# DeltaNet's 8x8 substitution on GpSimd instead of VectorE, and two weights' low halves on VectorE instead of GpSimd

## The chip, the cores and the metric

The kernel runs on one core of one Trainium2 chip. The metric is the device time of one execution in microseconds (us), the median over runs. The core's engines work side by side and wait for each other through semaphores: TensorE (PE, matrix products into PSUM), VectorE (DVE), ScalarE (ACT), GpSimd (POOL) and SyncE (SP), which issues the transfers from memory.

## The reference

A two-layer decoder over 272 tokens (16 learned ones and 256 of input), width 1024. Each layer is a half-step FFN, a mixer and another half-step FFN. The mixer projects its input once and splits the columns among three head groups: stick-breaking attention, gated DeltaNet and an S5 state-space group with a gated output (GLU). Cut to the part that the change touches, DeltaNet solves, for every head and chunk of tokens, a unit lower triangular system:

```
lmat  = where(strict, einsum('bhnid,bhnjd->bhnij', kb, kc) * decay, 0.0)
t_inv = triangular_solve(lmat + eye, eye, left_side=True, lower=True, unit_diagonal=True)
u = t_inv @ (vc * beta);   w = t_inv @ (kb * exp(gc))
attn = where(incl, (qc @ kc^T) * decay, 0.0)
# then over the chunks, in sequence: v_new = u - w S;  o = q exp(g) S + attn v_new
#                                    S = S exp(g_last) + (k exp(g_last - g))^T v_new
h += concat(o_sb, o_dn, o_s5) @ w_out
```

## The kernel before

**Products in three parts.** A weight tile comes from memory as fp32 (`raw`). `weights` (lines 127 to 141) makes a high half `wh` on ACT (L136) and a low half `wl = raw - wh` by one subtraction of 128x1024 (L139), on VectorE, or on GpSimd if the weight's number within the mixer is in `ON_POOL` (line 47). `mm3` (L144 to L146) adds three products: `wh xh`, `wh xl` and `wl xh`. A unit of the projection is 8 blocks of 3 products, 24 matmuls of 128x272.

**The mixer** (`mixer`). In the order in which it is run: the units of the convolution's columns (`conv`), of `s5u`, `z`, `q`, `k`, `v`. VectorE takes each unit out of PSUM (L1343, L1358, L1364). Meanwhile `dn_gates` makes DeltaNet's triangular matrices `LT`, and `s5` runs the state-space scan in four groups: PE gives `pinc` (L821), VectorE rotates, scans and rotates back (L825 to L839), and GpSimd clears the first column (L837) once L836 is done. When the projections are through come the attention's scores (`pz`, L1227 to L1231), DeltaNet's second set of products (`pl`, L887) and transposes (`pv`), S5's outputs (`pY`, L850 and L852), the GLU (`pglu`), the rest of the attention (L1242 to L1257) and the output projection.

**The inverse** (`dn_inverse`). Nine sets of four 8x8 diagonal blocks stand in each column of partitions. One product with `bd8` (`pl8` and `pl8t`, L992 and L994) spreads each block's entries over its partitions, ACT copies them out of PSUM as `Lb` (L996, L997). Then the 8x8 blocks are inverted by substitution: seven steps, each a product (L1005) and a subtraction (L1006) that needs the step before; L1008 spreads the result into 32x32 tiles `TT32`, and VectorE transposes them (L1010, `T32`). Two levels of block doubling follow, each `px` (L1016), a copy, `py` (L1022), a subtraction (L1024) and a transpose (L1025); then 32 to 64 (`px2`, `py2`, L1033 to L1054) and 64 to 128 (L1060 to L1071). Only then can `dn_rest` run its sequence over the chunks (`pvn` L1138, `pS` L1143 and L1145, `pk` L1129 and L1130).

**What sets the order.** The program is written in Python order with priorities (`first()` puts DeltaNet ahead of all, `second()` the GLU); a scheduler then orders the instructions of each engine once, when the kernel is built, by its own estimate of times. On the chip each engine takes its instructions strictly in that order: an instruction that must wait holds up all behind it.

Of the kernel before, what the change touches and what calls it, by code (L numbers as in the profile page):

```python
# [14 lines left out]
ALU = mybir.AluOpType  # L15
# [3 lines left out]
P = 128  # L19
# [24 lines left out]
HORD = (0, 1, 4, 2, 5, 3, 8, 6, 7, 9)  # L44
SA, SB = 1, 1
CONV, UORD, ZK = (0, 1, 4, 5), (0, 1, 2, 3), 0
ON_POOL = (5, 7, 10, 15, 20, 25)
NBUF = (3, 2, 3)
LO_POOL = 5

# [5 lines left out]
def bc(ap, axis, n):  # L56
    return ap.unsqueeze(axis).to_broadcast([*ap.shape[:axis], n, *ap.shape[axis:]])
# [6 lines left out]
class Trunk:  # L64
# [17 lines left out]
    def psum(self, tag, nm):  # L82

        return self.ps.tile([P, 512], F32, tag=tag, name=nm, bufs=2)
# [885 lines left out]
    def dn_inverse(self):  # L970

        nc = self.nc
        V, G, A, PE = nc.vector, nc.gpsimd, nc.scalar, nc.tensor
# [17 lines left out]
        p = psum("pl8")  # L991
# [3 lines left out]
        Lb = self.m1024("Lb")[:, :576]  # L995
        A.copy(Lb[:, :512], p)  # L996
        A.copy(Lb[:, 512:], p2[:, :64])  # L997
        Lb = Lb.rearrange("p (u i j) -> p u i j", u=9, i=8)
# [1 line left out]
        for k in range(2):  # L1000
            G.tensor_tensor(Lm[k], L32, bc(self.lev[k], 1, 9), op=ALU.mult)
        TT8, t8 = tl([P, 9, 8], "TT8"), tl([P, 9, 8], "t8")
        V.tensor_copy(TT8, bc(self.id8, 1, 9))
        for j in range(7):
            V.tensor_tensor(t8[:, :, j + 1:], Lb[:, :, j + 1:, j], TT8[:, :, j:j + 1].to_broadcast([P, 9, 7 - j]), op=ALU.mult)  # L1005
            V.tensor_tensor(TT8[:, :, j + 1:], TT8[:, :, j + 1:], t8[:, :, j + 1:], op=ALU.subtract)  # L1006
        TT32, T32 = t9("TT32"), t9("T32")
        V.tensor_tensor(TT32.rearrange("p u (b i) -> p u b i", b=4), bc(TT8, 2, 4),  # L1008
                        bc(self.m8c.rearrange("p (b i) -> p b i", b=4), 1, 9), op=ALU.mult)
        V.transpose(fl(T32), fl(TT32))  # L1010

        for k in range(2):
# [10 lines left out]
            Tn, TT32 = t9("T32"), t9("TT32")  # L1023
# [293 lines left out]
    def mixer(self, l, nxt):  # L1317
# [7 lines left out]
        R = self.R  # L1325
        self.on_pool, self.nw = ON_POOL, -1
        with ExitStack() as es:
# [167 lines left out]
```

## Time and profile before

| | us |
|---|---|
| median of 3 runs | 1191.51 (1189.88 to 1191.59) |
| profiled execution, its own time | 1194.31 |
| its span, first to last instruction | 1192.5 |
| PE busy in the span | 1154.8 (97%) |
| VectorE busy | 853.6 (72%) |
| ScalarE busy | 614.1 (52%) |
| GpSimd busy | 175.3 (15%) |

The mixer of layer 0 stands at about 227 to 410 us of the span, that of layer 1 at about 815 to 1000 us. The share of busy time is a mean over stages with different limits; the two mixers are where PE waits or runs at a low clock, and the windows below are taken from them.

### The profile page before, as it was taken

The numbers are of one execution on the slowest core, as the hardware profiler recorded it, in microseconds if no ns is written. First come the engines' busy times: TensorE is split into PE (matmuls) and PEld (weight loads), VectorE is DVE, ScalarE is ACT, GpSimd is POOL, SyncE is SP. The second block draws the span as 40 slices with busy tenths as digits, with TensorE's granted clock in tenths as the row PEclk, the third lists the DMA queues.
The fourth block names the chain that finished last, engine by engine and source line by source line (L and its number), as shares of the span: only waits on it lengthen the run. The fifth ranks groups of instructions, "written<-read, shape, count | busy, mean of one in ns | idle before, by whom it ended". The sixth has DMA issues, their size and how long they took to land.

```text
span 1192.5 us, 23762 instructions
## 1 busy us (share of the span) xinstructions
PE 1154.8 (97%) x9544; PEld 1104.5 (93%) x9544; DVE 853.6 (72%) x1648; ACT 614.1 (52%) x981; POOL 175.3 (15%) x210
## 2 busy tenths in 40 slices
PE   8999999999998999999999999999999989999997
PEld 7999999998786999999999999999988969999985
DVE  7999986699636866555579998756994268666644
ACT  6455575564166654444455556645632566555533
POOL 6312100021010111110201112011210001111100
PEclk9999999999789999999999999999997599999999
DMA  5656545543201455555565555455431015666663
GB/s 182 179 175 180 166 135 160 167 125 108 71 19 54 142 175 177 168 176 171 177 187 177 169 173 172 132 175 156 124 112 33 27 45 185 181 188 191 187 191 117
DMA packets 196858, 173.74 MB, mean 146 GB/s; under 512 B 21300, under 2 KB 193004, under 8 KB 196748
## 3 DMA queue, kind: packets, MB, share of 16 engines
q1 hardware_dynamic: 196732, 172.22, 48.2%
q8 instruction: 75, 1.23, 0.4%
q14 instruction: 35, 0.29, 0.1%
q10 hardware_dynamic: 16, 0.00, 0.0%
HBM read 171.15 MB, written 1.05 MB: 144 GB/s over the span
## 4 chain that ended last, share of the span: by engine, by line
PE 84%; DVE 10%; ACT 3%; issue 1%; DMA 1%; SPq 0%; ACTq 0%; DVEq 0%
PE proj L146 17%; PE proj L145 17%; PE proj L144 17%; PE pd L146 5%; PE pd L145 5%; PE pd L144 5%; PE pd L493 5%; DVE wl L139 2%; PE pY L852 1%; DVE qkv L1346 1%; DVE xT L1437 1%; PE pY L850 1%; PE pl L887 1%; PE pm L783 1%; PE pz L1227 1%
## 5 line engine op out<-in xcount | busy, mean ns | idle before, releaser
L144 PE MATMUL proj<-xh,wh 128*128 128x272 f32 (+1 forms) x1840 | 521.1, 289 | 6.3 <-DVE sy L1435 2.8
L145 PE MATMUL proj<-xl,wh 128*128 128x272 f32 (+1 forms) x1840 | 518.4, 287 | 0.2 <-DVE xl L1296 0.2
L146 PE MATMUL proj<-xh,wl 128*128 128x272 f32 (+1 forms) x1840 | 492.8, 290 | 3.3 <-DVE wl L139 3.0
L136 ACT ACTIVATE wh<-raw 128x1024 fp32r<-128x1024 f32 (+1 forms) x324 | 338.2, 1044 | 292.8 <-PE proj L145 99.5
L139 DVE TENSOR_TENSOR wl<-raw,wh 128x1024 fp32r<-128x1024 f32 (+1 forms) x312 | 378.4, 1213 | 146.6 <-PE pd L146 60.9
L144 PEld LDWEIGHTS proj<-xh,wh 128*128 128x128 f32 x1840 | 345.4, 188 | 10.5 <-DVE sy L1435 4.1
L145 PEld LDWEIGHTS proj<-xl,wh 128*128 128x128 f32 x1840 | 345.2, 188 | 3.0 <-issue 1.5
L146 PEld LDWEIGHTS proj<-xh,wl 128*128 128x128 f32 x1840 | 328.8, 187 | 7.2 <-DVE wl L139 5.8
L144 PE MATMUL pd<-hh,wh 128*128 128x272 f32 x528 | 149.6, 288 | 0.0
L145 PE MATMUL pd<-hl,wh 128*128 128x272 f32 x528 | 149.3, 288 | 0.0
L435 POOL TENSOR_TENSOR hl<-h,hh 128x272 fp32r<-128x272 f32 (+1 forms) x88 | 81.1, 924 | 452.9 <-ACT hh L434 452.8
L146 PE MATMUL pd<-hh,wl 128*128 128x272 f32 x528 | 140.8, 288 | 0.2
L144 PEld LDWEIGHTS pd<-hh,wh 128*128 128x128 f32 x528 | 99.2, 188 | 0.2
L145 PEld LDWEIGHTS pd<-hl,wh 128*128 128x128 f32 x528 | 99.3, 188 | 0.1
L146 PEld LDWEIGHTS pd<-hh,wl 128*128 128x128 f32 x528 | 95.1, 188 | 1.0 <-DVE wl L139 0.9
L107 ACT ACTIVATE g<-g 128x272 f32<-128x272 f32 (+2 forms) x92 | 37.6, 415 | 68.9 <-DVE g L429 68.8
L433 DVE TENSOR_TENSOR h<-proj,g 128x272 f32<-128x272 f32 (+1 forms) x88 | 37.7, 433 | 32.9 <-PE proj L146 21.3
L434 ACT ACTIVATE hh<-h 128x272 fp32r<-128x272 f32 (+1 forms) x88 | 36.4, 419 | 47.1 <-DVE h L433 47.1
L429 DVE TENSOR_TENSOR g<-proj,R 128x272 f32<-128x272 f32 (+1 forms) x88 | 37.5, 430 | 17.8 <-PE proj L146 17.6
L139 POOL TENSOR_TENSOR wl<-raw,wh 128x1024 fp32r<-128x1024 f32 x12 | 30.7, 2557 | 110.5 <-ACT th L107 34.9
L431 DVE TENSOR_TENSOR g<-g,R 128x272 f32<-128x272 f32 (+1 forms) x88 | 37.7, 432 | 12.6 <-ACT g L107 12.3
L376 POOL TENSOR_TENSOR acc<-acc,sq 128x272 f32<-128x272 f32 (+1 forms) x20 | 22.7, 1134 | 91.4 <-ACT sq L370 90.5
(490 smaller groups left out, 1310.1 us busy)
## 6 DMA issues: line engine op xcount, KB each, us to landing
raw<-in_ffn_w_gate_dram SPq DMA_DIRECT2D x88, 512.0 KB, 3.6
raw<-in_ffn_w_up_dram SPq DMA_DIRECT2D x88, 512.0 KB, 3.6
raw<-in_ffn_w_down_dram SPq DMA_DIRECT2D x70, 512.0 KB, 3.5
raw<-in_w_in_dram SPq DMA_DIRECT2D x36, 512.0 KB, 4.4
raw<-in_ffn_w_down_dram SPq DMA_DIRECT2D x24, 384.0 KB, 3.0
raw<-in_w_out_dram SPq DMA_DIRECT2D x16, 512.0 KB, 3.5
raw<-in_s_w_glu_dram SPq DMA_DIRECT2D x4, 512.0 KB, 3.4
xin<-in_x_dram SPq DMA_DIRECT2D x4, 256.0 KB, 5.8
```

The costliest lines, as they stand in the source:

```text
L107: i = self.nc.scalar.activation(out, in_, func, **k)
L136: nc.scalar.activation(h[:, :n], r[:, :n], AF.Copy)
L139: e.tensor_tensor(l[:, :n], r[:, :n], f32(h[:, :n]), op=ALU.subtract)
L144: mm(p, wh, xh, start=first, stop=False)
L145: mm(p, wh, xl, start=False, stop=False)
L146: mm(p, wl, xh, start=False, stop=last)
L429: V.tensor_tensor(g1, pg[j][:, :N], R, op=ALU.mult)
L431: V.tensor_tensor(g1, g1, R, op=ALU.mult)
L433: V.tensor_tensor(h, pu[j][:, :N], g1, op=ALU.mult)
L434: nc.scalar.activation(hh[:, f, :N], h, AF.Copy)
L435: G.tensor_tensor(hl[:, f, :N], h, f32(hh[:, f, :N]), op=ALU.subtract)
L493: PE.matmul(pd[i][e], x[:, f, ts], w[:, 0, e * 512:e * 512 + 512], start=f == 0 and w is h and x is hh, stop=f == NF - 1 and w is lo)
```

## The change

The substitution's 16 instructions per layer (the copy of the unit matrix, seven products, seven subtractions, and the spreading into 32x32 tiles) are issued on GpSimd instead of VectorE. The transpose that follows stays on VectorE. The weights 10 and 15 of each mixer (the first unit of `z`, and the second of `k`) leave `ON_POOL`, so that their low halves are made on VectorE. All lines from 1003 on move by one: L1005 of before is L1006 of the changed kernel, L1010 is L1011, L1016 is L1017.

```
-ON_POOL = (5, 7, 10, 15, 20, 25)
+ON_POOL = (5, 7, 20, 25)
...
-        V.tensor_copy(TT8, bc(self.id8, 1, 9))
+
+        G.tensor_copy(TT8, bc(self.id8, 1, 9))
         for j in range(7):
-            V.tensor_tensor(t8[:, :, j + 1:], Lb[:, :, j + 1:, j], TT8[:, :, j:j + 1].to_broadcast([P, 9, 7 - j]), op=ALU.mult)
-            V.tensor_tensor(TT8[:, :, j + 1:], TT8[:, :, j + 1:], t8[:, :, j + 1:], op=ALU.subtract)
+            G.tensor_tensor(t8[:, :, j + 1:], Lb[:, :, j + 1:, j], TT8[:, :, j:j + 1].to_broadcast([P, 9, 7 - j]), op=ALU.mult)
+            G.tensor_tensor(TT8[:, :, j + 1:], TT8[:, :, j + 1:], t8[:, :, j + 1:], op=ALU.subtract)
         TT32, T32 = t9("TT32"), t9("T32")
-        V.tensor_tensor(TT32.rearrange("p u (b i) -> p u b i", b=4), bc(TT8, 2, 4),
+        G.tensor_tensor(TT32.rearrange("p u (b i) -> p u b i", b=4), bc(TT8, 2, 4),
                         bc(self.m8c.rearrange("p (b i) -> p b i", b=4), 1, 9), op=ALU.mult)
         V.transpose(fl(T32), fl(TT32))
```

The scheduler orders every engine anew. Three places, all in the mixer of layer 0 (layer 1 reads the same but for numbers):

GpSimd's queue, as a difference (`s5z_3954` is the first S5 group's state, `s5z_3981` the second's):

```order
 L837 MEMSET s5z_3954 128x8
-L139 TENSOR_TENSOR wl<-raw,wh 128x1024
+L1006 TENSOR_TENSOR t_3313<-Lb,TT_3312 128x9x7
+L1007 TENSOR_TENSOR TT_3312<-TT_3312,t_3313 128x9x7
+L1006 TENSOR_TENSOR t_3313<-Lb,TT_3312 128x9x6
...
+L1007 TENSOR_TENSOR TT_3312<-TT_3312,t_3313 128x9
+L1009 TENSOR_TENSOR TT_3329<-TT_3312,m8c 128x288
 L837 MEMSET s5z_3981 128x8
```

The 15 instructions stand in one piece behind the clearing of the first S5 group's column, and nothing stands between them.

VectorE's queue around the transpose that closes the substitution, before (`pv` is the last unit of the projection, the rotations are those of the fourth S5 group):

```order
L1364 SCALAR_TENSOR_TENSOR pv<-proj,R 128x272
L825 TENSOR_TENSOR w<-pinc,cs 128x272
L826 SCALAR_TENSOR_TENSOR x<-pinc,sn 128x272
L827 TENSOR_TENSOR w<-pinc,cs 128x272
L828 TENSOR_TENSOR x<-pinc,sn 128x272
L1010 STREAM_TRANSPOSE T_3330<-TT_3329 128x288
L830 TENSOR_TENSOR s5z_4035<-w,x 128x544
```

and in the changed kernel (four rotations, L825 to L828, stand where a line of dots is):

```order
L836 TENSOR_TENSOR x<-s5z_3954,sn 128x544
L838 TENSOR_TENSOR s5z_3954<-w,x 128x4x67
L839 TENSOR_TENSOR s5z_3954<-w,x 128x4x67
...
L1365 SCALAR_TENSOR_TENSOR pq<-proj,R 128x272
L139 TENSOR_TENSOR wl<-raw,wh 128x1024
L830 TENSOR_TENSOR s5z_3981<-w,x 128x544
L1365 SCALAR_TENSOR_TENSOR pk<-proj,R 128x272
L139 TENSOR_TENSOR wl<-raw,wh 128x1024
L832 SCALAR_TENSOR_TENSOR s5z_3981<-dec,s5z_3981 128x272 x2
L1011 STREAM_TRANSPOSE T_3330<-TT_3329 128x288
```

The transpose moved up from the fourth S5 group to the second, and now waits for GpSimd; 13 VectorE instructions stand between L836, which lets GpSimd's chain begin, and it.

PE's queue around the first level's first product (`px`), before and then in the changed kernel (`proj_4325` is the first unit of `v`):

```order
L1231 MATMUL pz_4572<-pq_3709,pk_3710 16x16
L887 MATMUL pl_4077<-qkv_3074,kn_3239 128x128 x4
L1016 MATMUL px_3333<-T32_3330,Lm_3308 32x32 x36
L887 MATMUL pl_4083<-qkv_3074,kn_3239 128x128 x4
L891 MATMUL plt_4089<-qkv_3074,kn_3239 32x32 x4
```

```order
L145 MATMUL proj_4325<-xl_95,wh_4328 128x272
L146 MATMUL proj_4325<-xh_94,wl_4329 128x272
L144 MATMUL proj_4325<-xh_94,wh_4328 128x272
L1017 MATMUL px_3333<-T32_3330,Lm_3308 32x32 x36
L145 MATMUL proj_4325<-xl_95,wh_4328 128x272
```

The product moved from behind all projections, among the scores, into the projections of `v`. Between `pl8t` and it PE has 70 projection matmuls and 8 of `pinc`; behind it come 23 more, `py`, 8 of `pinc`, 12, the second level's `px` and 6, and with these the projections end. In the same way `pvn`, `pS`, `pk` and the second `pvn` of `dn_rest` moved ahead of the first `pglu`, into the stretch of `pY`.

## Rows read from the trace of the kernel before

**Rows 1.** Windows: us, then busy time (instructions) of each engine, PE clock, DMA.

```profile
285.00:308.00 23.00, 18.89 (x143) 17.36 (x141) 23.00 (x52) 5.58 (x7) 3.44 (x4) 0.99 0.36 115
308.00:325.00 17.00, 16.86 (x292) 13.99 (x292) 9.17 (x20) 1.17 (x5) 0.11 (x1) 0.51 0.10 33
343.00:382.00 39.00, 36.10 (x262) 29.96 (x262) 22.12 (x48) 25.21 (x52) 3.05 (x2) 0.93 0.18 55
873.00:897.00 24.00, 19.68 (x153) 18.25 (x152) 24.00 (x55) 5.95 (x7) 3.41 (x4) 1.00 0.38 118
926.00:946.00 20.00, 19.57 (x101) 18.40 (x101) 4.38 (x13) 7.75 (x18) 2.35 (x1) 0.50 0.02 6
```

**Rows 2.** Timeline of VectorE, layer 0: start us, us, instruction.

```profile
283.46 0.23 DVE L1005 TENSOR_TENSOR t<-Lb,TT 128x63 f32<-128x63 f32 x1
...
290.83 0.70 DVE L830 TENSOR_TENSOR s5z<-w,x 128x544 f32<-128x544 f32 x1
...
291.58 1.33 DVE L832 TENSOR_TENSOR_SCAN s5z<-dec,s5z 128x272 f32<-128x272 f32 x2
...
295.50 1.21 DVE L139 TENSOR_TENSOR wl<-raw,wh 128x1024 fp32r<-128x1024 f32 x1
296.64 0.43 DVE L825 TENSOR_TENSOR w<-pinc,cs 128x272 f32<-128x272 f32 x1
...
305.37 0.45 DVE L1008 TENSOR_TENSOR TT<-TT,m8c 128x288 f32<-128x288 f32 x1
...
308.61 0.47 DVE L1010 STREAM_TRANSPOSE T<-TT 128x288 f32<-128x288 f32 x1
```

**Rows 3.** Chain that ended last, layer 0: start us, us, what.

```profile
299.42 1.73 PE pinc L821 x16
...
315.20 1.11 PE px L1016 x72
...
320.59 1.12 PE py L1022 x72
...
327.45 0.75 PE py L1022 x54
...
364.23 0.38 PE pS L1143 x8
364.61 1.03 PE pS L1145 x8
...
408.43 0.38 PE proj L144 x3
```

**Rows 4.** Timeline of VectorE and of GpSimd where both read SBUF.

```profile
265.17 2.95 DVE L1346 SCALAR_TENSOR_TENSOR qkv<-pad,prm,qkv 128x272 f32<-128x272 f32 x2
...
286.55 3.10 POOL L139 TENSOR_TENSOR wl<-raw,wh 128x1024 fp32r<-128x1024 f32 x1 [1.42 <-PE proj L146]
...
288.08 1.64 DVE L1006 TENSOR_TENSOR TT<-TT,t 128x54 f32<-128x54 f32 x1
```

**Rows 5.** GpSimd's groups by form: shapes, count, busy us, mean ns, idle before.

```profile
L139 POOL TENSOR_TENSOR wl<-raw,wh 128x1024 fp32r<-128x1024 f32 x12 | 30.7, 2557 | 110.5 <-ACT th L107 34.9 <-DVE qkv L1346 32.5 <-issue 23.6
...
L235 POOL COPY lev<-mkVB 32x32 f32<-32x32 f32 x4 | 3.3, 814 | 4.6 <-DVE mkVB L228 4.5
...
L376 POOL TENSOR_TENSOR acc<-acc,sq 128x256 f32<-128x256 f32 x2 | 1.6, 796 | 1.6 <-ACT sq L370 1.5
```

**Rows 6.** Instructions on line 994, both layers: duration ns, first and last start.

```profile
L994 PE MATMUL pl8t<-r,bd x4: 219/247/275, 279.8 to 867.9; 128*128 128x64 f32 x4
```

**Rows 7.** Timeline of PE, layer 0: start us, us, instruction.

```profile
307.36 0.54 PE L1216 MATMUL pvs<-ident,pv 128*128 128x128 f32 x2 [2.11 <-DVE pv L1364]
...
354.21 0.43 PE L1129 MATMUL pk<-qkv,kn 64*128 64x64 f32 x2
...
355.43 0.38 PE L1130 MATMUL pk<-qkv 64*128 64x64 f32 x2
359.67 1.08 PE L1138 MATMUL pvn<-ds,TTf 128*128 128x64 f32 x8 [0.16 <-DVE ds L1135]
```

## The prediction

> **What bounds the kernel now.** [...] I read windows over a mixer first, then the chain of waits inside them, then the engines' timelines. From 285 to 308 us, the end of the projections, VectorE is busy for 23.0 of 23 us and PE for 18.9; in layer 1 for 24 of 24, and PE for 19.7 [rows 1]. VectorE is the limit there, and PE loses 4.1 and 4.3 us. [...]
>
> [...]
>
> **The change, part by part (one layer; layer 1 reads alike).**
>
> *VectorE.* The substitution leaves it; two subtractions of 1.21 us come to it [rows 2], and two of GpSimd's go. That matters, since the engines hold each other up: `qkv` L1346 takes 2.95 us for two and L1006 takes 1.64 us, the latter until GpSimd's `wl` (286.55 and 3.10) is through at 289.65 [rows 4]. Undisturbed, two of 272 elements at 0.43 and one of 63 at 0.23 [rows 2] make 0.86 and 0.2, so 2.1 and 1.4 were lost. [...] VectorE's balance: minus 3.5 of stalls, minus about 2 for the 16 instructions (an instruction starts 0.07 before the last one ends, as 296.64 does against 295.50 and 1.21, so each is at most 0.16, and L1008 is 0.38), plus 2.3. It gains 3 us, less what the chain costs it.
>
> *GpSimd's chain.* No row shows a small GpSimd product. A line through 796 ns at 256 elements and 2557 ns at 1024 [rows 5] gives 0.21 us plus 2.29 ns an element. The 14 instructions have 63 to 9 elements a partition, 504 together: 14 x 0.21 + 504 x 0.00229 = 4.1 us; L1009 with 288 is 0.9. Below that I see nothing, so 5.0 is the lower end. The upper end is the dearest small row, a copy of 32 elements at 814 ns [rows 5]: 14 x 0.814 + 0.9 = 12.3. I take 7, nearer the products' line, since each step must wait for the last one's semaphore.
>
> *Is the transpose ready when VectorE comes to it?* The chain starts when L836 is through. From there VectorE has 13 instructions to L1011: two subtractions, two scans, one sum, and eight of 272 elements: 2 x 1.21 + 1.33 + 0.70 + 8 x 0.43 = 7.9 by rows, less 0.07 of overlap each, so 7.0 [rows 2]. [...] So both arrive together at about 9.5 us, and `T32` stands some 10 us after L836. What queues behind L1011 is serious: all of S5's scans, and the subtraction for `v`'s second unit, for which PE waits.
>
> *PE to the end of the projections.* `pl8t` stood at 279.8 to 280.05 [rows 6]; ahead of it come 25 more projection matmuls at 0.127 and 5 `pinc` at 1.73 / 8 [rows 3], so it ends at 284.3. Then 70 and 8 of these, 10.6 us: PE wants `px` at 294.9. L836 stood one instruction of 544 elements behind the first L1005, so it was through about 284.9; one subtraction has been pulled ahead of it, 286.0; so `T32` comes at 296: a wait of 1.1. Then 23 matmuls, `py`, 8 `pinc`, 12 matmuls, `px`, 6 matmuls: 41 x 0.127 + 1.7 + 2 x 0.75 = 8.4, and the first `px` 0.75, giving 305.2. The second `px` needs a transpose 10.4 us of VectorE's queue behind L1011, at 306.4, when PE is at 303.7: a wait of 2.7. The projections end at about 307.9, and `pn`, the next step, stands at 308.6, where it stood at 308.1 (behind the `pvs` of 307.36) [rows 7]. So three products enter this stretch at the price of 0.5 us: they fill waits that were there anyway. Without waits the same sum ends 3.3 earlier; if the chain needs 5 us more, 5 later.
>
> *PE behind the projections.* [...] `px2` and `py2` come into the slow part: by the ratio 1.1 / 0.75 on about 1.6 us, plus 0.75. `dn_rest`'s first half now stands before the GLU: `pvn` twice at 1.08, `pS` 0.38 + 1.03, `pk` 1.60 from first to last [rows 3, 7], 5.2 us; so the GLU starts 0.5 - 3.3 + 0.75 + 5.2 = 3.2 later, and GLU and attention lose 5.2 of PE's work. What is this worth there? PE is busy for 36.1 of 39 us in that stretch [rows 1], so most of it; at least `pvn` and `pS` (2.5 to 2.9), which stand on the chain itself. I take 4.7.
>
> *The sum.* Per layer 0.5 - 3.3 + 0.75 + 5.2 - 4.7 = -1.55; twice, -3.1. Against the profiled execution's 1194.31 that is 1191.2; against the median of the runs, 2.8 lower, 1188.4.
>
> **The rivals.**
>
> *The chain is too slow (slower).* Place: L1011, with VectorE's whole queue behind it and PE at `px` and at the second `px`. At the upper end, 12.3 us, the transpose comes 5.3 later, and nothing takes that up, since VectorE has no idle time there. Per layer 5.3 - 1.55 = +3.75, 1199. [...] For it: the contention above, and the order, built from estimates that put PE, VectorE and GpSimd at this point almost together. Against it: GpSimd stands idle around the chain, and its clean rows lie on one line.
>
> *Nothing gained.* `dn_rest`'s products were cheap where they stood, between waits of the GLU for ACT; only 2.9 of 5.2 come back. Per layer 0.5 - 3.3 + 0.75 + 5.2 - 2.9 = +0.25: 1192. For it: VectorE and ACT are busy 22 and 25 of those 39 us, and the GLU alternates among three engines.
>
> *The clock.* The granted clock fell behind the stretch in which PE waited, and was 0.51 from 308 to 325; in layer 1 it was 0.50 again from 926 to 946, in `pY` and the first of the GLU [rows 1]. [...] But the products that used to be spread now stand in one block of small ones, and a longer slow part is as well possible: 1198. [...]
>
> **How the numbers follow.** My forecast, 1188.4, has a chance of 0.42; its own range is 1184 to 1192, from the ends of the waits and of the 4.7. The slow chain has 0.16, nothing gained 0.20, the clock kept up 0.13, a longer slow clock 0.09. About 0.2%, 2.4 us, is what a measurement tells from no change. Faster than 1189.1: most of the forecast's share and the better clock, 0.47. Within: 0.25, from the forecast's upper end and the second rival. Slower: the slow chain, the worse clock and a little of the second, 0.28. From 1178 to 1199 all but the ends of the clock and of the slow chain are in.
>
> **What would show it.** GpSimd's 15 instructions in one run of 7 to 10 us; VectorE's wait at L1011 under 2 us, and no instruction of 2.95 or 1.64 us in the stretch; `px` among the projections, with PE's two waits near 1 and 3 us; `pn` within 2 us of where it was; the GLU 3 us later and the output projection 1.5 us earlier. I am wrong if VectorE waits at L1011 for more than 4 us, if `pn` moves by more than 3 us either way, or if the slices at a clock of 0.5 change in number.

## The result: slower by 2.8%

The changed kernel takes 1223.33 us (median, 1221.87 to 1224.91), the kernel before 1190.7 beside it: 1.028 times as long, 95% interval 1.0255 to 1.0302. The forecast was 1188.4 and the range ended at 1199.

**What the change itself does came as worked out.** GpSimd's timeline, layer 0 (start us, us, instruction): first and last of the chain, and its two dearest pieces.

```profile
285.66 0.55 POOL L1006 TENSOR_TENSOR t<-Lb,TT 128x63 f32<-128x63 f32 x1
...
288.67 1.12 POOL L1007 TENSOR_TENSOR TT<-TT,t 128x36 f32<-128x36 f32 x1
...
290.90 1.10 POOL L1006 TENSOR_TENSOR t<-Lb,TT 128x18 f32<-128x18 f32 x1
...
293.59 0.80 POOL L1009 TENSOR_TENSOR TT<-TT,m8c 128x288 f32<-128x288 f32 x1
```

From 285.66 to the end of the last piece (293.59 and 0.80, 294.39) are 8.7 us. VectorE then waits a little at L1011:

```profile
291.82 1.37 DVE L832 TENSOR_TENSOR_SCAN s5z<-dec,s5z 128x272 f32<-128x272 f32 x2
294.43 0.48 DVE L1011 STREAM_TRANSPOSE T<-TT 128x288 f32<-128x288 f32 x1 [1.24 <-POOL TT L1009]
```

TensorE (PE) has the second `px` among the last projections and reaches `pn` 1.1 us earlier than before (it stood at 308.14, behind the `pvs` of [rows 7]). The second `py` still stands behind `pn`:

```profile
303.74 0.82 PE L1017 MATMUL px<-T,Lm 32*32 32x32 f32 x72 [0.23 <-DVE T L1025]
...
307.06 0.58 PE L1089 MATMUL pn<-bd,sq 128*128 128x2 f32 x4 [1.32 <-DVE x L826]
...
309.03 1.18 PE L1023 MATMUL py<-X,TT 32*32 32x32 f32 x72
```

**What went wrong lies behind `pn`.** The windows give us, busy time and instructions of PE, PEld, DVE, ACT and POOL, then PE's granted clock. First three of the kernel before, beside [rows 1]. Its clock was low from 308 to 324.5 and from 342 to 349 us, and in layer 1 from 898 to 912 and from 926 to 950:

```profile
340.00:345.00 5.00, 4.16 (x34) 3.90 (x33) 1.92 (x5) 3.32 (x9) 1.80 (x1) 0.67 0.00 0
345.00:350.00 5.00, 5.00 (x34) 4.86 (x32) 0.16 (x1) 1.05 (x3) 0.09 (x1) 0.65 0.00 0
897.00:911.00 14.00, 14.00 (x276) 11.20 (x276) 7.37 (x16) 1.16 (x3) 0.11 (x1) 0.54 0.09 28
```

The changed kernel:

```profile
285.00:309.00 24.00, 22.30 (x375) 20.94 (x373) 22.42 (x42) 6.17 (x8) 7.92 (x18) 0.99 0.38 112
309.00:370.00 61.00, 60.57 (x462) 54.98 (x462) 15.25 (x41) 13.77 (x36) 4.67 (x7) 0.50 0.03 10
370.00:380.00 10.00, 8.14 (x67) 6.59 (x66) 6.70 (x12) 8.96 (x16) 1.60 (x1) 1.00 0.31 105
863.00:917.00 54.00, 52.31 (x668) 49.28 (x670) 51.74 (x101) 24.55 (x39) 10.57 (x21) 0.99 0.40 115
917.00:970.00 53.00, 52.57 (x369) 47.46 (x362) 12.58 (x32) 12.17 (x33) 1.64 (x5) 0.50 0.04 11
```

The stretch at 0.50 behind `pn` is 61 us in layer 0 instead of 17, and 53 in layer 1 instead of two of 14 and 24. PE is shown busy for 60.57 of the 61. VectorE and ACT have 15 and 14 us of work there: nothing else is the bound. The clock row of the page (40 slices of 30.6 us, tenths of full speed) has 5 5 8 and 5 6 where the page of before, shown first, has 7 8 9 and 7 5:

```profile
PEclk9999999999789999999999999999997599999999
PEclk9999999999558999999999999999995699999998
```

The chain that ended last, layer 0 (start us, us, what), shows what the half clock costs piece by piece:

```profile
346.11 0.63 PE pS L1144 x8
346.74 1.90 PE pS L1146 x8
...
360.61 0.82 PE pglu L144 x2
```

and PE's timeline shows the second `pvn`:

```profile
358.27 1.91 PE L1139 MATMUL pvn<-ds,TTf 128*128 128x64 f32 x8
```

`pS` is 0.63 and 1.90 and `pvn` 1.91; in the kernel before `pS` was 0.38 and 1.03 [rows 3] and `pvn` 1.08 [rows 7]. The GLU's first product stands at 360.61, 53.5 us behind `pn`. In the kernel before (PE timeline) that was 35.0:

```profile
308.14 0.99 PE L1088 MATMUL pn<-bd,sq 128*128 128x2 f32 x4 [0.25 <-DVE x L826]
...
343.14 0.82 PE L144 MATMUL pglu<-xh,wh 128*128 128x272 f32 x2 [0.84 <-ACT xh L1278]
```

The clock comes back only at 370, among the GLU's products of 128x272 (in layer 1 at 970.6, 2.7 us behind the GLU's first). From `pn` to the GLU layer 0 loses 18.5 us and layer 1 16.4 (53.6, from 914.41 to 967.96, against 37.2, from 896.21 to 933.38).

### The profile page after: what moved, and what is told of

It is laid out like the page before. It is cut to its first block, busy times and chain, and to the rows that moved or that the text cites. A ratio compares the mean times of both kernels' runs of the same rounds, so it can differ in the third digit from the quotient of the medians.

```text
span 1223.1 us, 23761 instructions
## 1 busy us (share of the span) xinstructions
PE 1187.1 (97%) x9544; PEld 1131.3 (92%) x9544; DVE 850.2 (70%) x1620; ACT 614.6 (50%) x981; POOL 181.2 (15%) x238
## 4 chain that ended last, share of the span: by engine, by line
PE 84%; DVE 8%; ACT 3%; DMA 2%; issue 1%; POOL 1%; SPq 0%; ACTq 0%; DVEq 0%; POOLq 0%
PE proj L146 16%; PE proj L145 16%; PE proj L144 16%; PE pd L146 5%; PE pd L145 5%; PE pd L144 5%; PE pd L493 5%; DVE wl L139 2%; PE pY L852 2%; PE pY L850 1%; PE pl L887 1%; DMA raw<-in_ffn_w_gate_dram 1%; PE pm L783 1%; POOL t L1006 1%; PE pz L1228 1%
## 5 line engine op out<-in xcount | busy, mean ns | idle before, releaser
L139 DVE TENSOR_TENSOR wl<-raw,wh 128x1024 fp32r<-128x1024 f32 (+1 forms) x316 | 383.8, 1215 | 154.9 <-PE pd L146 60.9
L139 POOL TENSOR_TENSOR wl<-raw,wh 128x1024 fp32r<-128x1024 f32 x8 | 20.9, 2614 | 150.0 <-ACT th L107 61.2
```

The costliest lines, as they stand in the source:

```text
L139: e.tensor_tensor(l[:, :n], r[:, :n], f32(h[:, :n]), op=ALU.subtract)
```

## The experiments

All against the kernel before on the same chip. Theory A was: behind `pn` the clock falls in either kernel; what brought it back in the kernel before was the dense work that stood there, of which `px` and `py` are a part, and the change takes them away. The rivals: the low halves (B), mere wandering of the clock (C), something other than PE's own products (D).

### One part of the change at a time

e1: the chain on GpSimd, with `ON_POOL = (5, 7, 10, 15, 20, 25)` as before. e2: `ON_POOL = (5, 7, 20, 25)` alone, the chain on VectorE.

> The chain of the 8x8 blocks on GpSimd, the two low halves left on GpSimd as in the kernel before. Theory A (the clock falls at the end of the projections, and the inverse's 32x32 products, which in the kernel before stood behind that point and after which its clock rose, now stand ahead of it): here too px, py, px stand among the projections, so behind their end come only small products and the clock should stay at 0.50 up to the GLU: over 1205 us, 40 us or more at 0.50 in each layer. Rival B (the two low halves on VectorE, through the order they make): without them the time falls back to 1188 to 1194 us and the clock to about 17 us at 0.50. Rival C (the clock wanders by itself): no bound, but a repeat would spread by more than 1%.

> Only the two low halves on VectorE; the chain stays on VectorE as before. Theory A: px, py, px stay behind the projections' end, between pz, pl and pv, as in the kernel before, so the clock comes back within some 20 us: 1186 to 1196 us. Rival B (the low halves are the cause): about 1220 us and 50 to 60 us at 0.50 in each layer.

e1: 1205.61 us, ratio 1.0148 (1.0079 to 1.0217). e2: 1189.44, ratio 0.999 (0.9961 to 1.0019). So the low halves alone cost nothing, and the chain alone costs about half of the 2.8%; with both parts together it is the whole. Rival C falls as well: all 75 executions of the kernel before on record lie between 1187.84 and 1206.14 us, the four of the changed kernel above 1221. In e1 real projection products stayed behind `pn`, and in layer 0 of this execution the clock came back at 320, where 40 us or more at 0.50 were expected; in layer 1 it came up for 3 us at 911 and then stayed down to 955:

```profile
310.00:320.00 10.00, 9.57 (x116) 8.70 (x116) 7.75 (x18) 2.08 (x5) 1.75 (x5) 0.50 0.21 64
320.00:360.00 40.00, 37.43 (x360) 33.74 (x358) 15.09 (x35) 23.39 (x50) 4.19 (x2) 1.00 0.14 41
900.00:911.00 11.00, 11.00 (x104) 10.15 (x103) 6.64 (x15) 1.90 (x4) 0.57 (x2) 0.52 0.16 49
915.00:955.00 40.00, 40.00 (x200) 36.98 (x199) 3.58 (x11) 11.41 (x30) 0.00 (x0) 0.50 0.00 1
```

### Work left out

e7 is the kernel before without the two levels, e9 the changed kernel without them, e10 the changed kernel without the outer steps.

```
-        for k in range(2):
+        for k in range(0):          # e7, e9
             px = psum("px")
-        px = psum("px2")            # e10: px2, py2, px3, px4, py3 and their copies removed
```

> The kernel before without the two levels px, py, px, py of the inverse (left out of the computation, so T32 is only the 8x8 blocks' inverse from there on); nothing is moved ahead of the projections' end. Behind pn its TensorE order is then that of the changed kernel: pz, pl, px2, py2, pv, px3, px4, pY with pvn, pS and pk among it. The four left-out sets took some 4 to 5 us a layer. Theory A: without them nothing brings the clock back behind the projections' end: 0.50 for 40 us or more in each layer, 1203 to 1218 us although work is left out. Rival B (the clock hangs on the low halves, the GpSimd chain or the engines' waits): the clock is back as before, 1178 to 1186 us.

> The changed kernel without the two levels px, py, px, py (left out of the computation, as in the earlier run on the kernel before). With the chain on GpSimd they stood ahead of the projections' end, under the projections' clock. Theory A: leaving them out takes nothing from the stretch behind pn, so the clock stays as low there as in the changed kernel, 100 us or more at 0.50 in both layers; the four sets' 3 to 4 us a layer are saved at most: 1213 to 1224 us. Rival (the changed kernel's loss comes from where these sets stand among the projections): 1185 to 1195 us.

> The changed kernel without the outer steps of the inverse, px2, py2, px3, px4 and py3 with their copies (left out of the computation; the two levels px and py stay where the change puts them, ahead of the projections' end). Behind pn come then pl, one py, pz, pz, the eight pv in one piece, pvn, pY. Theory A (px and py are missing behind the fall): the clock stays at 0.50 there, 100 us or more in both layers; the left-out products saved some 9 us a layer at the low clock: 1200 to 1212 us. Theory F (the outer steps are what hurts: 16 sparse products of 1.0 to 1.9 us each set, which the change has moved in among pz, pl and pv, so that the pieces of dense work there are cut up): the clock comes back at the eight pv, some 12 to 16 us behind the fall, and 60 us or less of 0.50 are left in both layers: 1165 to 1182 us.

e7: **1221.56 us**, ratio 1.0263 (1.0241 to 1.0285). Four sets of products are taken out of the kernel before, nothing is moved to GpSimd, and it becomes as slow as the changed kernel. Its windows:

```profile
310.00:365.00 55.00, 54.56 (x362) 50.65 (x360) 10.86 (x27) 10.37 (x28) 1.92 (x2) 0.50 0.00 1
365.00:375.00 10.00, 9.66 (x82) 7.91 (x81) 7.61 (x15) 7.41 (x13) 2.40 (x1) 0.85 0.17 54
915.00:965.00 50.00, 49.85 (x337) 45.76 (x337) 10.40 (x26) 9.17 (x25) 0.42 (x2) 0.50 0.00 1
```

This is the sharpest run: the low stretches (307 to 368 and 915 to 969 us) are those of the changed kernel. It came out 3.6 us above the top of the expectation, but against rival B's 1178 to 1186 there is no doubt. With the sets gone the scheduler also orders the rest anew, so e7 shows that what stands behind `pn` decides, not yet that the sets do.

e9: 1216.83 (1201.36 to 1218.61), ratio 1.019 (1.0126 to 1.0254), 6.5 us less than the changed kernel: where the sets stood among the projections cost little. Its profiled execution is the fastest of its four (granted clock 0.959, the others 0.945). There the clock of layer 0 came back at 323.3, right behind `pz` and eight `pv` in one piece, with neither `px` nor `py` of the two levels in the kernel; in layer 1 it stayed down:

```profile
308.00:322.00 14.00, 13.90 (x82) 10.99 (x83) 8.13 (x18) 1.39 (x4) 0.11 (x1) 0.50 0.12 39
323.00:350.00 27.00, 26.62 (x259) 24.92 (x257) 9.72 (x25) 11.56 (x30) 4.21 (x2) 0.99 0.00 1
895.00:945.00 50.00, 49.56 (x281) 45.18 (x280) 13.04 (x34) 9.84 (x27) 0.11 (x1) 0.50 0.02 8
```

e10: 1211.69, ratio 1.0147 (1.0059 to 1.0235). The change does push the outer steps into that stretch, but without them the clock stays down as well, in layer 0 behind the same `pz` and eight `pv` (317.58 to 319.55):

```profile
309.00:355.00 46.00, 45.47 (x247) 41.02 (x246) 10.99 (x32) 10.59 (x29) 3.13 (x5) 0.50 0.04 12
910.00:955.00 45.00, 44.56 (x235) 40.45 (x235) 9.93 (x30) 10.10 (x28) 1.10 (x4) 0.50 0.02 6
```

### Products added for the clock alone

Twelve bfloat16 products of 128x512, whose result the next real product overwrites: e3 in the first `pY` bank, e5 in the first `pl` bank behind `pn`.

```
+                for _ in range(12):
+                    PE.matmul(p, self.identb, bc(self.negl, 1, 4), start=True, stop=True)
```

> The changed kernel with 12 added bfloat16 products of 128x512 columns (identity times a constant) into the first pY bank, which pY's own products then overwrite; the order around them is the same. Theory A says that the stretch behind pvt is slow only for want of dense products: the clock should rise at or soon behind these 12 (some 5 us at the low clock), pY's sets go from 1.28 to about 0.67 us, the GLU starts 8 to 14 us earlier in each layer less the 3 to 5 us added: 1198 to 1214 us. Rival D (what holds the clock is not PE's own products, but the wait on dn_rest's results or the other engines): the clock stays at 0.50 to the GLU and the time grows by twice 5 us, to about 1233 us.

> The changed kernel with the 12 added bfloat16 products of 128x512 put right behind pn, into the first pl bank of dn_rest, some 17 us earlier than in the run before. Theory A: the clock falls at about 309 us as in the changed kernel, the 12 take about 5 us at the low level, the clock is back by 315 us (325:330 in the run before) and stays up through pz, pv and pY, so the GLU starts at about 341 to 346 us (360.6 without them): 1184 to 1197 us. Rival D (these products raise the clock only where pY follows): it falls again behind them, 1200 to 1215 us.

e3: 1201.37 us (1200.94 to 1201.88), ratio 1.0082 (1.0054 to 1.011): 22 us faster than the changed kernel with more to compute. The clock rose while they ran (327.80 to 331.62 us; 0.50 up to 330, 1.00 from 331) and held through `pY` and `dn_rest`'s products, so D falls:

```profile
309.00:329.00 20.00, 20.00 (x223) 15.37 (x214) 8.80 (x21) 2.92 (x8) 2.08 (x5) 0.50 0.09 28
330.00:350.00 20.00, 18.82 (x176) 17.39 (x174) 1.73 (x6) 8.16 (x22) 1.80 (x1) 0.99 0.00 1
350.00:360.00 10.00, 8.93 (x79) 8.21 (x74) 6.44 (x14) 4.22 (x10) 2.39 (x1) 0.83 0.04 10
```

e5: 1199.78, ratio 1.0075 (1.0053 to 1.0098), not the 1184 to 1197 expected. The clock was back by 311, while they ran, then fell again inside `pY`, in layer 0 soon behind `px3` and `px4` (16 products of 32 columns in 1.11 us each set):

```profile
308.00:311.00 3.00, 3.00 (x78) 1.58 (x77) 3.00 (x7) 0.00 (x0) 0.00 (x0) 0.53 0.40 134
311.00:327.00 16.00, 16.00 (x210) 12.91 (x208) 7.38 (x18) 4.57 (x12) 1.65 (x5) 1.00 0.03 10
328.00:360.00 32.00, 32.00 (x155) 30.14 (x155) 5.20 (x12) 9.80 (x24) 4.22 (x2) 0.50 0.00 1
```

So `pY` did not raise the clock there (0.50 from 328 to 360 us) and did not always hold it (1.00 up to 327). The same products in the kernel before:

> The same 12 products in the kernel before. [...] Theory A: 1186 to 1198 us, with the second low stretch of layer 1 gone. Rival D: 1196 to 1201 us, the low stretches as before.

> The same 12 products behind pn in the kernel before, whose clock comes back at 324.5 us by itself. Theory A: it comes back some 5 to 8 us earlier; the 12 cost about 5 us at the low level; what is left is small: 1186 to 1197 us.

e3's twelve: 1199.85 us, ratio 1.0068 (1.0045 to 1.0092), above theory A's 1186 to 1198; the second low stretch of layer 1 shrank from 24 us to 10 (937 to 947) and did not go. e5's twelve: 1194.36, ratio 1.0029 (1.0002 to 1.0057), as expected; the clock came back at 316 instead of 324.5. There the clock comes back by itself, so the added work is mostly loss.

### Dense or small work put back behind `pn`

e6 adds four products ahead of `pn`, which makes the scheduler leave groups of projections behind it; e8 holds the chain back on GpSimd; e4 adds 108 products of 32x32.

```
+                    PE.matmul(warm[:, :TP], self.bd64, sq, start=True, stop=True)     # e6, x4
+            G.tensor_tensor(Lm[1], L32, bc(self.lev[1], 1, 9), op=ALU.mult)           # e8, x20
+                            PE.matmul(p[s, x * 32:x * 32 + 32], self.ident[s, s], self.ident[s, s], start=True, stop=True)  # e4, x108
```

> The changed kernel with four added products of 128x288 on pn's first input, ahead of pn, into a bank of the projections. Their place in the order holds the last projections back: 7 or more groups of three projection products now stand behind pn, between pl, pv and px2. Theory A: dense products stand behind the fall without any being added there, so the clock comes back (or does not fall) before pY: 40 us or more of 0.50 per layer are gone, 1185 to 1203 us. Rival B: order among these does not matter, 1215 us or more.

> The changed kernel with its GpSimd chain held back: 20 repeats of the product that makes Lm[1] (0.8 to 1.3 us each, the same result each time) stand ahead of it on GpSimd, so T32 comes at 310 to 320 us instead of 295. The first px and py then stand at the projections' end and the second px and py behind pn, pz and pl, near where the kernel before has them. TensorE waits 3 to 13 us a layer for the late T32. Theory A: the clock comes back behind the second px and py, so the later chain makes the kernel faster than the changed one by 10 to 28 us: 1195 to 1213 us. Rival B (the chain on GpSimd as such, or the low halves, cost the time): the wait is added to it, 1229 to 1249 us.

> The changed kernel with 108 added 32x32 products (three times the 36 of one px, on the identity) in the first pl bank behind pn. Theory A2 (it is the small products of px and py, standing close together, that brought the clock back in the kernel before): the clock is back behind them, some 5 us after their start, though the inverse's waits for px2 and py2 now stand among them; if it then holds to pY's end 1190 to 1203 us. Rival E (only wide products bring it back, and px and py had the place of something else): 0.50 from 309 to 365 us as in the changed kernel, about 1225 to 1235 us.

e6: 1202.44 us, ratio 1.0108 (1.0084 to 1.0132), as expected, though by another way in part: up behind the projections, down again in `pY`, where layer 0 spent 27 us at 0.50 and layer 1 31.

e8 is a miss, between the two forecasts: 1223.05, ratio 1.0252 (1.0181 to 1.0324). The second `px` and `py` stood behind the fall, and the clock stayed at 0.50 for 54 us. PE's timeline in e8, and then in the kernel before up to where its clock came back (324.5):

```profile
319.29 1.27 PE L1230 MATMUL pz<-pq,pk 64*128 64x272 f32 x2
...
320.97 1.18 PE L1019 MATMUL px<-T,Lm 32*32 32x32 f32 x72
322.08 3.09 PE L887 MATMUL pl<-qkv,kn 64*128 64x128 f32 x16
...
325.61 1.18 PE L1025 MATMUL py<-X,TT 32*32 32x32 f32 x72
...
328.03 1.06 PE L1036 MATMUL px<-T,LT 32*32 32x32 f32 x32
```

```profile
318.50 1.27 PE L1227 MATMUL pz<-pq,pk 64*128 64x272 f32 x2
...
320.52 1.19 PE L1022 MATMUL py<-X,TT 32*32 32x32 f32 x72
321.64 0.47 PE L1101 MATMUL pv<-ident,qkv 128*128 128x128 f32 x1
...
323.70 1.12 PE L1016 MATMUL px<-T,Lm 32*32 32x32 f32 x72
```

Before, `pz`, `py`, eight `pv` (321.64 to 323.6) and `px` follow one another; in e8 the sets stand apart, with 3.09 us of 64-row `pl` and the sparse `px2` between.

e4: 1220.78, ratio 1.0293 (1.0212 to 1.0373), 4 us below rival E's forecast. In layer 0 the 108 small products, with PE's waits for the outer steps among them, did not raise the clock. In layer 1 it fell at 924.3 and came back at 944.7, behind eight `pv` in one piece (942.41 to 944.3), 9 us behind the last of the small products:

```profile
308.00:371.00 63.00, 59.52 (x673) 53.89 (x664) 15.30 (x40) 12.36 (x34) 3.95 (x6) 0.50 0.03 10
925.00:940.00 15.00, 13.01 (x292) 12.17 (x293) 6.03 (x14) 1.91 (x5) 2.15 (x5) 0.50 0.10 33
```

So small products did not raise the clock wherever they stood (it was 0.50 for 54 us in e8 and for 63 in e4's layer 0). With the close train of `pz`, `py`, `pv` and `px` in place the clock came back in both layers of the kernel before and of e2. With three or all four of the `px` and `py` sets out of that stretch it stayed down in both layers of the changed kernel, e7 and e10. It is not shown that the train needs them: the same `pz` and eight `pv` without them brought the clock back in layer 0 of e9's profiled execution, and did not in e10's. Which part of the train is enough, and how surely, stays open.

### Versions

> The changed kernel with 6 added bfloat16 products of 128x512 in the first pl bank and 3 ahead of each of the four pY sets, 18 a layer: 3.9 us at 0.217 us each if the clock is up. Theory A: the clock falls only briefly behind pn and stays up through pY; against the 126 us at 0.50 in the two layers of the changed kernel 90 or more go, each worth half a microsecond, less 8 to 10 us of added products: 1180 to 1194 us. If 6 do not bring it back ahead of pz: 1194 to 1206 us.

> The changed kernel with 12 added products behind pn and 4 ahead of each pY set, 28 a layer (6.1 us at 0.217 us each). The run with 6 and 3 came out at 1184 to 1234 us from one execution to the next; if 12 make the first rise certain the spread goes: 1180 to 1192 us in all executions; if the later ones are what fails it spreads again.

> The changed kernel with 12 added 128x512 products behind pn and 8 ahead of py3, behind px3 and px4, where the clock fell again in the run with 12 alone. Theory A: up from about 312 us to the GLU in both layers, 25 us or less at 0.50 in each: 0.47 us for each of the 75 us that go, less 9 us of added products: 1182 to 1194 us. If the clock falls in pY again: 1197 to 1208 us.

> The same 18 products a layer in the kernel before, which stood at 0.50 for about 24 and 38 us in its two layers. If two thirds of that go, 20 us are won and 8 to 10 us paid: 1176 to 1188 us. If the products only replace what its own did: 1194 to 1202 us.

> The kernel before with 12 in the first pl bank and 3 ahead of each pY set, 24 a layer. Two of the earlier runs had 12 there and their clock came back some 5 us behind their start, then fell again in pY of layer 0. With the three of each pY set it should stay up: 15 us or less at 0.50 in each layer, 1176 to 1190 us.

The changed kernel with 6 and 3 spread from 1183.68 to 1233.61 us over four executions, with a granted clock of 0.986 to 0.943; they lie too far apart for a ratio. With 12 and 4: 1190.07 (1180.79 to 1204.42, ten executions), ratio 0.9981 (0.9951 to 1.0011). With 12 and 8: 1193.9, ratio 1.001 (0.9977 to 1.0042). The kernel before with 6 and 3: 1201.84, ratio 1.0076; with 12 and 3: 1200.81, ratio 1.008; both some 10 us slower. The first lies in the forecast for products that only replace what its own did, the second missed. None beats the kernel before; the one with 12 and 4 gives back all that the change lost. Of the changed kernel's versions only 12 and 8 came within its forecast; with 12 and 4, five of ten executions did. The fastest with 12 and 4 (1180.79, clock 0.990) says what a steadier clock would be worth here; its later falls, here in the profiled execution of 1195.81, are what spreads it:

```profile
308.00:325.00 17.00, 17.00 (x256) 11.94 (x255) 10.22 (x22) 2.65 (x7) 1.64 (x5) 0.90 0.11 33
326.00:339.00 13.00, 13.00 (x64) 10.86 (x64) 0.84 (x2) 3.49 (x9) 0.00 (x0) 0.50 0.01 1
```

## Why the prediction was wrong

**Right.** The chain (7 us alone, 9.5 with 2.5 allowed for VectorE and GpSimd holding each other up; 8.7 measured), VectorE's wait at L1011 (1.24), the two stalls of 2.95 and 1.64 [rows 4] gone (a `qkv` of the first takes 0.49 now), `px` among the projections, and `pn` within 2 us (1.1 earlier, for 0.5 later). That `pn` came out so near is in part luck: of PE's two waits, forecast at 1.1 and 2.7 us, the first did not come and the second was 0.23; a wait of 1.32 for L826 stood ahead of `pn` instead. The rival of a chain too slow did not come. No run shows the 2.5 as a term: with the chain beside them VectorE's 13 instructions up to L1011 took 7.6 us (285.57 to 293.19) where 7.0 was worked out, and the chain took 1.7 more than its 7. Between one step and the next GpSimd stood idle for 0.08 us, 1.1 in all.

**Wrong: the step "PE behind the projections".** The -3.3 of the sum stands for `px`, `py` and the second `px`, which leave the stretch behind `pn`, at the 1.1 us that each took there ([rows 3]: 1.11 and 1.12). It counted them as cost and nothing else, and no run shows it as a gain. The 0.75 in the ratio 1.1 / 0.75 is 54 instructions of the fourth set [rows 3]; all 72 took 0.82 at 1.00 (PE timeline, 327.38). The terms -3.3, +0.75 and +5.2 made +2.65 us from `pn` to the GLU, on the understanding that the clock there would be what [rows 1] showed. Measured: +18.5 and +16.4, since the clock stayed at 0.50 up to the GLU. e7 takes the four sets out of the kernel before, with the order that follows from it, and loses 31 us. The prediction's last sign of being wrong came: the clock row has three slices at 5 where it had one.

The prediction had this as a rival, "a longer slow part", with 0.09 and a size of +10 us for both layers together. It was sized by one of the stretches of 17 and 20 us of [rows 1]; the low stretch grew by 44 in layer 0 alone. The row to read was there: [rows 1 and 3] have the clock at 0.51 with PE busy for 16.86 of 17 us, so being busy did not by itself bring it back; the `py` behind 325 ran at 1.00 again, so the question was what had ended the low stretch, and the change moves three sets out of it. The prediction names the fall behind PE's wait and the 0.51 from 308 to 325, and did not ask what ended it. Its other rival on the clock, the one kept up (0.13), did not come either: low time grew in both layers.

Where wide products were put in for a test, the clock rose while they ran: to 1.00 by 331 us in e3, by 311 in e5. In the changed kernel it stayed at 0.50 for 61 us of which the profile shows PE busy for 60.57.

**The 4.7 to come back in GLU and attention** can't be read off. From the GLU's first product to `po` layer 1 was 4.1 us shorter (38.3 against 42.4), but its clock was higher there (0.92 against 0.81, some 10 us less at 0.50). Layer 0 was 1.4 longer (41.0 against 39.6) at a lower clock (0.80 against 0.93, some 11 us more at 0.50). Nor did all of the 5.2 move in layer 1: in the kernel before, one `pvn` stood ahead of the GLU there already (931.04 against 933.38).

**How much is the clock?** Low time is twice (1 - granted clock) times span: 67 us before and 132 after. A line through span and low time gives 0.36 us for a microsecond at 0.50 among the 71 executions of the kernel before that ran beside the experiments, and 0.46 among the ten of the version with 12 and 4. So the 65 us more are an estimated 23 to 30 of the 30.6 us between the two spans. The rest, 1 to 7 us, is not settled; `dn_rest`'s products ahead of the GLU are one candidate.

## What to carry to other kernels

Where PE's clock falls and comes back in a stretch, ask which products it came back behind before moving any of them. In e7 leaving work out made the kernel 2.6% slower, so a product can be worth more than its own time. Read more than one execution before you name the product: e9's four gave two answers. PE's busy share did not tell it here (60.57 of 61 us at 0.50); the granted clock by windows did, and a dozen wide products put in for a test showed within one run that the slow stretch was slow by its clock (e3, 22 us faster).

## What the runs showed of the hardware

- The quickest of the small GpSimd products lie on the line drawn from larger ones (0.21 us and 2.29 ns an element): 54 elements 0.32, 45 elements 0.30, 9 elements 0.22 us. Two took 1.1 (36 and 18 elements), each while a subtraction of 128x1024 ran on VectorE (288.36 for 1.32 us, 290.65 for 1.25).
- The 128x512 bfloat16 products took 0.45 us each at 0.50 (e5's order in the kernel before, 3.60 us for eight) and 0.22 at 1.00 (6 and 3, from the start of three at 324.06 to the next product's at 324.71).
- The same program can go either way: the four executions with 6 and 3 differed by 50 us, in step with the granted clock (0.986 to 0.943).
- The same `pY` products ran on at 1.00 in the kernel before (325 to 341) and on at 0.50 in the changed kernel (328 to 358): a set took 0.67 or 1.28 us.
